# Fillers between SBUF pools, a token-major last projection, and 64x64 steps on four quarters of the array

## The chip, the cores and the metric

The kernel runs on one core of a Trainium2 chip. The metric is the device time of one execution in microseconds; the time of a kernel is the median over runs. An execution is also recorded by the hardware profiler, which gives the start and length of each instruction on five engines: TensorE (PE, and PEld for its weight loads), VectorE (DVE), ScalarE (ACT), GpSimd (POOL) and SyncE (SP), which issues most transfers.

## What is computed

A trunk of two decoder layers over 256 tokens of 2048 channels. Layer 0 mixes by stick-breaking attention and a gated delta rule, layer 1 by latent attention and gated linear attention; both go on with cross-attention to a memory of 256 rows and a convolutional feed-forward network (FFN) of 5632 hidden channels. Cut to what the change touches:

```python
def conv_ffn(h, w_in, conv_w, conv_b, w_out):
    uz = causal_dwconv(h @ w_in, conv_w) + conv_b
    u, z = jnp.split(uz, 2, axis=-1)
    return (jax.nn.silu(z) * u) @ w_out
...
    # gated_delta_rule, chunks of c = 64 tokens
    t_inv = jnp.eye(c, dtype=f32) + neg_n
    p = neg_n
    for _ in range(c.bit_length() - 2):
        p = p @ p
        t_inv = t_inv + t_inv @ p
...
    for layer in range(DEPTH):
        hn = rmsnorm(h, norm_mix[layer])
        ...
        h = h + memory_cross_attention(rmsnorm(h, norm_xattn[layer]), mem_n, ...)
        h = h + conv_ffn(rmsnorm(h, norm_ffn[layer]), ffn_w_in[layer], ...)
    return rmsnorm(h, final_norm)
```

## The kernel before

**Layout.** Activations lie channel-major: a tile has 128 channels on the partitions and the 256 tokens along the row. The residual stream is the 16 tiles X[0] to X[15].

**Exactness.** Every float32 factor is split into a rounded high part and a low remainder, and the products high x high, high x low and low x high are summed. An activation tile of 512 columns (xs, hid, mix, ms) holds 256 high and 256 low columns side by side. `get` brings half a slab of weights (128 x 1024) by a transfer on SP's queue into one of five raw buffers; ACT casts it to hi (L240), DVE subtracts to get lo in two halves (L249, from `low`). Four buffers of hi and of lo run ahead of TensorE.

**The main loop.** `mm_tile` keeps a 128x128 block of weights stationary and moves activations: for each block one matmul of 512 columns with hi (L277) and one of 256 with lo (L278), summed in a PSUM tile g. These two are called a pair here. `gemm` does 16 pairs for one output tile of 128 channels. `mm_narrow` does the same with three matmuls of 256 columns (L287 to L289). `gemm_b` is the other way about: a 128-token tile of activations is stationary and 512 weight columns move, three matmuls for each k and token tile (L326, L327, L329); it makes token-major results, in the value projections alone.

**The FFN.** `ffn` works in four groups of 11 hidden tiles. `into` makes a group: 22 output tiles of 16 pairs each, convolution, silu, product, and the split result hid0 to hid10. `out` then multiplies the group by the second weight matrix: 16 output tiles of 11 pairs, each added to X by `residual` (L416, L418). The last tile of all uses `mm_narrow`.

**The end.** `Final.feed` squares each finished X tile and multiplies it by the gain (ACT), POOL sums the squares; after the last tile TensorE sums over the partitions (L388), `rsqrt` works on 128x256 elements, 16 multiplications (L1264) follow, and eight transfers (L1265) write the channel-major result, which is transposed after the run.

**The delta rule.** `delta_pair` handles two heads; each head has two tiles t of two 64-token chunks. In six steps `it` it squares a 64x64 matrix and accumulates the inverse. Both chunks of a tile lie on the diagonal quarters of the array: rows and columns 0 to 63, and 64 to 127 (`halves`). For each step the code issues head 0's eight matmuls (L671 or L673, then L678 or L680), then head 1's; ACT copies (L692) and DVE adds (L694).

**Order.** Such side work is a generator; `Side` advances it as the pairs go by (`side.tick`, a `yield n` is n ticks), and the framework's scheduler then orders the instructions of each engine from its own estimates, so neighbours in the code need not be neighbours on the engine. Each engine runs its list in that order.

**Memory.** Pools are laid out one after another: constants and X (cp), xs and the like (xp), weights raw, hi, lo (wp), temporaries (tp), then the pools of a stage (mix's, the FFN's fp). A tile's size is rounded up to 32 bytes a partition, so a pool's start modulo 128 follows from what lies before it.

Of the kernel before, what the change touches and what calls it, by code (L numbers as in the profile page):

```python
# [10 lines left out]
F32 = mybir.dt.float32  # L11
# [7 lines left out]
P = 128  # L19
# [6 lines left out]
FG = 4  # L26
# [12 lines left out]
for _name, _c in SLABS:  # L39
# [6 lines left out]
    ("nm0", 16), ("nm1", 16), ("nx0", 16), ("nx1", 16), ("nf0", 16), ("nf1", 16), ("mem", 16), ("fin", 16),  # L46
# [101 lines left out]
def build(tc, nc, a):  # L148
# [87 lines left out]
    def part(raw):  # L236

        n = raw.shape[-1]
        hi, lo = parts()
# [5 lines left out]
    def parts():  # L245
        return [wp.tile([P, 1024], F32R, name=n, bufs=4) for n in ("hi", "lo")]
# [6 lines left out]
    def get(i, h, keep=None):  # L253
        if (i, h) not in cache:
# [7 lines left out]
            cache[i, h] = part(raw)  # L262
# [91 lines left out]
    class Norm:  # L354


        def __init__(self, d, name="R", bufs=2, p=None, cols=False):
            self.d, self.name, self.bufs, self.p, self.r = d, name, bufs, p, None
            self.acc, self.last, self.cols = {}, [], cols
# [22 lines left out]
        def get(self):  # L382
            if self.r is None:
                n = 258 if self.cols else 256
                ps = acc()
                z = list(self.acc.values()) + self.last
# [55 lines left out]
    def even():  # L442
# [143 lines left out]
        def delta_pair(h0, kq0s, vs, sgts):  # L586
# [63 lines left out]
            for i in two:  # L650
# [5 lines left out]
                for r in halves:  # L656
                    V.tensor_tensor(out=n[r, :, 2], in0=p3[r, :, r], in1=C["I64"][r, 0:64].unsqueeze(1).to_broadcast([64, 2, 64]), op=ALU.add)
                sts.append(n)
            yield 6

            full = [None, None]
            for it in range(6):
                p2s = [acc() for _ in two]
                c0, c1 = (1 if it < 4 else 2), (3 if it > 0 else 2)
                for i in two:
                    p3 = p2s[i][:, 0:384].rearrange("p (t c) -> p t c", t=2)
                    st = sts[i]
                    for t in range(2):
                        for r in halves:
                            if it == 0:  # L670
                                T.matmul(p3[r, t, 64:128], lhsT=p0[i][r, t, r], rhs=pt[i][r, t, r], start=True, stop=True)  # L671
                            else:
                                T.matmul(p3[r, t, 64 * c0:64 * c1], lhsT=st[r, t, 0], rhs=st[r, t, c0:c1], start=True, stop=True)  # L673
                    if it < 5:
                        for t in range(2):
                            for r in halves:
                                if it == 0:
                                    T.matmul(p3[r, t, 0:64], lhsT=pt[i][r, t, r], rhs=p0[i][r, t, r], start=True, stop=True)  # L678
                                else:
                                    T.matmul(p3[r, t, 0:64], lhsT=st[r, t, 1], rhs=st[r, t, 0], start=True, stop=True)  # L680
                for i in two:
                    p3 = p2s[i][:, 0:384].rearrange("p (t c) -> p t c", t=2)
                    st = sts[i]
                    if it == 5:
                        full[i] = vec("U")
                        G.memset(full[i], 0.0)
                        for r in halves:
                            V.tensor_tensor(out=full[i][r, :, r], in0=p3[r, :, 128:192], in1=st[r, :, 2], op=ALU.add)
                        continue
                    n = st if it == 0 else e("st", (P, 2, 3, 64), 4)  # L690
                    c = 2 if it < 4 else 1
                    A.copy(n.rearrange("p t q n -> p t (q n)")[:, :, 0:64 * c], p3[:, :, 0:64 * c])  # L692
                    if it:
# [489 lines left out]
    def ffn(l, nxt, after):  # L1183
        fp, es = open_pool("fp")
        e = maker(fp)
        xs, nm = nxt.xs, nxt.nm
# [29 lines left out]
        def out(gi, hid, nxt=None):  # L1216
            for n in range(16):
                ps = psum_g()
                f = [(gi * 16 + n) * FJ + k for k in range(FJ)]
                last = l == 1 and gi == FG - 1 and n == 15  # L1220
# [160 lines left out]
```

## Time and profile before

| | |
|---|---|
| time, median of 3 runs | 2589.1 us (2588.49 to 2589.78) |
| the profiled execution | 2590.2 us |
| its span, first to last instruction | 2588.4 us |
| TensorE matmuls | 15195, on 99% of the span |
| read from HBM | 453.28 MB, 176 GB/s |
| transfers of 512 KB of weights | 845, 3.3 us to landing each |

The page gives busy times, the chain of work that ended last (each step followed back to what released it), and groups of equal instructions: line, engine, operation, output and inputs, count, then busy time, mean length in ns, and idle time ahead of them with its releasers. Lengths of matmuls overlap, since a matmul starts before the one ahead has drained; what a matmul costs is the distance between starts. The FFNs run from 645 to 1373 us and from 1834 to 2574 us of the span.

### The profile page before, as it was taken

What the parts mean: (1) busy time and instruction counts of PE and PEld (TensorE: products, weight loads), DVE (VectorE), ACT (ScalarE), POOL (GpSimd) and SP (SyncE); (2) the same over time, 40 slices, a digit from 0 to 9 for tenths busy, and PEclk for the clock granted to TensorE, in tenths of its full rate; (3) what the DMA queues carried; (4) which work ended last, traced back from release to release, by engine and by line L of the source; (5) the groups of instructions that cost most, each with busy time, mean ns of one, the idle gap of its engine ahead of it and who ended that gap; (6) DMA issues with size and microseconds to landing.
All of it is one profiled execution on the core that took longest, in us unless ns stands there. A gap on an engine that the chain in (4) does not pass through costs nothing.

```text
span 2588.4 us, 41299 instructions
## 1 busy us (share of the span) xinstructions
PE 2560.0 (99%) x15195; PEld 2228.8 (86%) x15195; DVE 1972.0 (76%) x4050; ACT 1485.5 (57%) x2522; POOL 175.6 (7%) x240
## 2 busy tenths in 40 slices
PE   9999999999999999999999999999999999999997
PEld 7888888888888888888888888888988888888886
DVE  8888776877877767767777677876877777777766
ACT  7677656655655545545456555755655545535544
POOL 2001000302000000000011012120200000000001
PEclk9999999999999999999999999999999999999999
DMA  7333345654555555555555544465555555555553
GB/s 244 127 119 123 123 153 173 211 180 157 195 189 193 188 188 187 189 187 186 190 188 185 188 159 151 141 210 171 172 190 192 188 193 184 186 193 183 185 195 123
DMA packets 127548, 458.08 MB, mean 177 GB/s; under 512 B 14288, under 2 KB 14928, under 8 KB 127344
## 3 DMA queue, kind: packets, MB, share of 16 engines
q1 hardware_dynamic: 126000, 453.59, 52.7%
q8 instruction: 119, 1.95, 0.3%
q10 hardware_dynamic: 1344, 1.84, 0.2%
q14 instruction: 85, 0.70, 0.1%
HBM read 453.28 MB, written 2.10 MB: 176 GB/s over the span
## 4 chain that ended last, share of the span: by engine, by line
PE 92%; DVE 5%; ACT 2%; issue 1%; POOL 0%; DMA 0%; SPq 0%; DVEq 0%; ACTq 0%; POOLq 0%
PE g L277 53%; PE g L278 27%; PE g L326 2%; PE g L329 2%; PE g L327 2%; DVE lo L249 2%; DVE xs L231 1%; PE ps_a L673 1%; DVE cv L548 1%; DVE X L416 0%; ACT hi L240 0%; PE ps_a L1170 0%; PE ps_a L613 0%; PE ps_a L680 0%; PE ps_a L1135 0%
## 5 line engine op out<-in xcount | busy, mean ns | idle before, releaser
L249 DVE TENSOR_TENSOR lo<-raw,hi 128x512 fp32r<-128x512 f32 (+1 forms) x1697 | 1172.2, 705 | 477.0 <-ACT hi L240 462.7
L277 PE MATMUL g<-xs,hi 128*128 128x512 f32 x4112 | 1457.1, 398 | 2.3 <-DVE xs L231 2.1
L240 ACT CAST hi<-raw 128x1024 fp32r<-128x1024 f32 (+1 forms) x847 | 888.9, 1051 | 821.6 <-PE g L277 528.7
L278 PE MATMUL g<-xs,lo 128*128 128x256 f32 x4112 | 1154.7, 281 | 0.0
L277 PEld LDWEIGHTS g<-xs,hi 128*128 128x128 f32 x4112 | 771.7, 188 | 184.0 <-DVE xs L231 4.2
L278 PEld LDWEIGHTS g<-xs,lo 128*128 128x128 f32 x4112 | 776.0, 189 | 2.7 <-DVE lo L249 0.6
L277 PE MATMUL g<-hid,hi 128*128 128x512 f32 x1397 | 484.6, 392 | 0.0
L278 PE MATMUL g<-hid,lo 128*128 128x256 f32 x1397 | 390.5, 280 | 0.0
L277 PEld LDWEIGHTS g<-hid,hi 128*128 128x128 f32 x1397 | 262.3, 188 | 58.0
L278 PEld LDWEIGHTS g<-hid,lo 128*128 128x128 f32 x1397 | 262.3, 188 | 0.0
L370 POOL TENSOR_TENSOR sqacc<-sqacc,sq 128x256 f32<-128x256 f32 x129 | 115.7, 901 | 1981.6 <-ACT sq L369 1974.8
L277 PE MATMUL g<-mix,hi 128*128 128x512 f32 x508 | 178.6, 394 | 0.0
L1198 DVE SCALAR_TENSOR_TENSOR fc<-y,cg,fc 128x255 f32<-128x255 f32 x352 | 168.0, 478 | 0.1
L278 PE MATMUL g<-mix,lo 128*128 128x256 f32 x508 | 142.1, 280 | 0.0
L337 DVE TENSOR_TENSOR y<-g,t 128x256 f32<-128x256 f32 x285 | 118.7, 417 | 4.7 <-ACT t L335 4.2
L416 DVE TENSOR_TENSOR X<-g,X 128x256 f32<-128x256 f32 x192 | 80.2, 419 | 47.9 <-PE g L278 41.7
L277 PEld LDWEIGHTS g<-mix,hi 128*128 128x128 f32 x508 | 95.2, 187 | 22.6
L335 ACT COPY t<-g 128x256 f32<-128x256 f32 x285 | 103.1, 362 | 6.4 <-PE g L278 6.1
L1196 ACT ACTIVATE fc<-y,cg 128x256 f32<-128x256 f32 x176 | 105.3, 599 | 2.2 <-DVE y L1194 2.2
L278 PEld LDWEIGHTS g<-mix,lo 128*128 128x128 f32 x508 | 95.2, 187 | 0.0
L1194 DVE TENSOR_TENSOR y<-y,R 128x256 f32<-128x256 f32 x176 | 73.3, 417 | 0.1
L230 ACT ACTIVATE xs<-X,cg 128x256 fp32r<-128x256 f32 x96 | 47.6, 506 | 40.2 <-DVE X L418 25.6
(357 smaller groups left out, 2295.7 us busy)
## 6 DMA issues: line engine op xcount, KB each, us to landing
raw<-w SPq DMA_DIRECT2D x845, 512.0 KB, 3.3
raw<-mem SPq DMA_DIRECT2D x8, 512.0 KB, 3.5
X<-x SPq DMA_DIRECT2D x8, 256.0 KB, 5.7
out<-xg SPq DMA_DIRECT2D x4, 256.0 KB, 2.3
out<-xg ACTq DMA_DIRECT2D x4, 256.0 KB, 2.5
raw<-w SPq DMA_DIRECT2D x2, 384.0 KB, 5.1
cg<-cg SPq DMA_DIRECT2D x1, 599.5 KB, 8.9
raw<-w SPq DMA_DIRECT2D x2, 256.0 KB, 4.4
```

The costliest lines, as they stand in the source:

```text
L240: A.copy(hi[:, 0:n], raw)
L249: V.tensor_tensor(out=lo[:, s], in0=raw[:, s], in1=f32(hi[:, s]), op=ALU.subtract)
L277: T.matmul(ps[0:m, 0:512], lhsT=hi[:, w], rhs=xs[k], start=first and q == 0, stop=False)
L278: T.matmul(ps[0:m, 0:256], lhsT=lo[:, w], rhs=xs[k][:, 0:256], start=False, stop=last and q == n - 1)
L326: T.matmul(ps[t], lhsT=xh, rhs=hi[:, w], start=k == 0, stop=False)
L335: A.copy(t[0:m], ps[0:m, 256:512])
L337: V.tensor_tensor(out=y[0:m], in0=ps[0:m, 0:256], in1=t[0:m], op=ALU.add)
L370: eng.tensor_tensor(out=self.acc[eng], in0=self.acc[eng], in1=q, op=ALU.add)
L416: V.tensor_tensor(out=X[n], in0=ps[:, 0:256], in1=X[n], op=ALU.add)
L1194: V.tensor_tensor(out=y, in0=y, in1=R, op=ALU.mult)
L1196: A.activation(c, y, AF.Identity, scale=col(f"fc{l}", n * 3 + 2), bias=col(f"fb{l}", n))
L1198: V.scalar_tensor_tensor(out=c[:, s:], in0=y[:, 0:S - s], scalar=col(f"fc{l}", n * 3 + 2 - s), in1=c[:, s:], op0=ALU.mult, op1=ALU.add)
```

## The change

Three things are changed. First, unused tiles (`fill`) of 32, 96 and 64 bytes are put into the pools xp, wp and tp, and 64 into the second FFN's pool; hi and lo get 1056 columns for 1024, and where weights move, the data starts 8 columns (32 bytes) in (`skew`). With the 16 gain columns that leave the constants this sets the addresses modulo 128 bytes: xs from 0 to 96, hi and lo from 0 to 64, hid from 32 to 96, and mix at 96.

```diff
+    def fill(p, n):
+        p.tile([P, n // 4], F32, name="fill", bufs=1)
+    fill(xp, 32)
+    fill(wp, 96)
+    fill(tp, 64)
+    SKEW = 8
-        hi, lo = parts()
+        hi, lo = [x[:, skew:skew + n] for x in parts()]
-        return [wp.tile([P, 1024], F32R, name=n, bufs=4) for n in ("hi", "lo")]
+        return [wp.tile([P, 1056], F32R, name=n, bufs=4) for n in ("hi", "lo")]
...
-            hi, lo = get(base + k // 4, k % 4 // 2)
+            hi, lo = get(base + k // 4, k % 4 // 2, skew=SKEW)
```

Second, the second FFN's output projection is token-major. `turn` transposes X into two token tiles XB during the first group; `out_b` replaces `out`: for each of four column tiles c of 512 channels and each k, three matmuls for each of two token tiles, weights moving. `finish` squares with a sum along the row, multiplies by the gain, and after the last column tile works out the norm on 128x1 elements, scales and writes rows of the result. In the last column tile the first token tile's last six k come ahead of the second's.

```diff
+        def turn():
+            for c in range(4):
+                for t in range(2):
+                    yield 6
+                    ps = acc()
+                    for i in range(4):
+                        T.transpose(ps[:, i * P:i * P + P], X[4 * c + i][:, t * P:t * P + P], ident)
+                    A.copy(XB[t][:, c], ps)
+            side.spawn(turn())
...
+            for c in range(4):
+                ps = [psum_g() for _ in range(2)]
+                steps = [(k, t) for k in range(FJ) for t in range(2)]
+                if end and c == 3:
+                    steps.sort(key=lambda s: (min(s[0], FJ - 6), s[1], s[0]))
+                for k, t in steps:
...
+                    T.matmul(ps[t], lhsT=xh, rhs=hi[:, w], start=k == 0, stop=False)
+                    T.matmul(ps[t], lhsT=xh, rhs=lo[:, w], start=False, stop=False)
+                    T.matmul(ps[t], lhsT=xl, rhs=hi[:, w], start=False, stop=k == FJ - 1)
+                    if k == FJ - 1:
+                        x = XB[t][:, c]
+                        V.tensor_tensor(out=x, in0=ps[t], in1=x, op=ALU.add)
+                        if end:
+                            finish(t, c, x)
...
+            q = e("fq", (P, 512), 2)
+            A.activation(q, x, AF.Square, accum_out=sums[:, t, c:c + 1])
+            o = xp.tile([P, 512], F32, name="xg", tag="xs", bufs=16)
+            (V if c == 3 else G).tensor_tensor(out=o, in0=x, in1=gb[:, c], op=ALU.mult)
+            fin[t, c] = o
+            if c == 3:
+                n = tmp("n", (P, 1), 2)
+                V.tensor_reduce(out=n, in_=sums[:, t], axis=AX.X, op=ALU.add)
+                z = rsqrt(n, 1, 1.0 / D, r[:, t:t + 1])
+                for i in range(4):
+                    o = fin[t, i]
+                    if i % 2:
+                        A.activation(o, o, AF.Identity, scale=z)
+                    else:
+                        V.tensor_scalar(out=o, in0=o, scalar1=z, scalar2=None, op0=ALU.mult)
+                    (nc.scalar if i % 2 else nc.sync).dma_start(a["out"][t * P:t * P + P, i * 512:i * 512 + 512], o)
```

Third, in `delta_pair` head 1's matrices change halves at each step (rows r, columns and output w = the other half), so that its matmuls use the two quarters of the array off the diagonal, and the code interleaves the heads.

```diff
+                for t in range(2):
+                    for i in two:
+                        for b in range(2):
+                            r, w = halves[b], halves[b ^ i]
...
+                                T.matmul(p2s[i][w, t, 64 * c0:64 * c1], lhsT=sts[i][r, t, 0], rhs=sts[i][r, t, c0:c1], start=True, stop=True)
...
+                        elif it and i:
+                            V.tensor_tensor(out=n[w, :, 2], in0=p3[w, :, 128:192], in1=st[r, :, 2], op=ALU.add)
-                    if it:
+                    if it and it < 5 and i == 0:
                         V.tensor_tensor(out=n[:, :, 2], in0=p3[:, :, 128:192], in1=st[:, :, 2], op=ALU.add)
```

In the order of TensorE, the second pair of heads (st holds a head's matrices, p_1909 head 1's first one, xs the gemm's activations), before:

```order
L671 MATMUL ps_a<-pt,p_1909 64x64 x4
L678 MATMUL ps_a<-p_1909,pt 64x64 x4
L673 MATMUL ps_a<-st 64x128 x4
L680 MATMUL ps_a<-st 64x64 x4
L278 MATMUL g<-xs_209,lo 128x256
L673 MATMUL ps_a<-st 64x128 x4
L680 MATMUL ps_a<-st 64x64 x4
L277 MATMUL g<-xs_216,hi 128x512
```

and the same place now:

```order
L683 MATMUL ps_a<-pt,p_1916 64x64 x4
L691 MATMUL ps_a<-p_1916,pt 64x64 x4
L685 MATMUL ps_a<-st 64x128 x4
L693 MATMUL ps_a<-st 64x64 x4
L288 MATMUL g<-xs_212,lo 128x256
L685 MATMUL ps_a<-st 64x128 x4
L693 MATMUL ps_a<-st 64x64 x4
L287 MATMUL g<-xs_219,hi 128x512
```

The lines have moved (L673 is now L685, L680 is L693, L277 is L287), the order has not: four matmuls of one head follow each other, on two quarters. In the fourth pair of heads, now:

```order
L685 MATMUL ps_a<-st 64x128 x8
L693 MATMUL ps_a<-st 64x64 x8
L288 MATMUL g<-xs_226,lo 128x256
L287 MATMUL g<-xs_233,hi 128x512
L288 MATMUL g<-xs_233,lo 128x256
L287 MATMUL g<-xs_240,hi 128x512
L685 MATMUL ps_a<-st 64x128 x4
L693 MATMUL ps_a<-st 64x64
L685 MATMUL ps_a<-st 64x128 x4
L693 MATMUL ps_a<-st 64x64 x7
```

Here eight follow each other, of both heads, on four quarters; that holds for three steps of this pair. In all, the steps stand in 35 runs between the gemm's matmuls where they stood in 34.

On DVE, the end of the program before (rs_v, rs_q and R are the norm's values, xg the results):

```order
L343 TENSOR_SCALAR rs_v<-ps_a 128x256
L349 SCALAR_TENSOR_TENSOR rs_q<-rs_q,rs_v 128x256
L351 SCALAR_TENSOR_TENSOR R<-rs_q,rs_y 128x256
L1264 TENSOR_TENSOR xg_26823<-xg_26823,R 128x256 x2
L1264 TENSOR_TENSOR xg_26903<-xg_26903,R 128x256 x2
```

with six more such rows behind these, and now:

```order
L1298 TENSOR_SCALAR xg<-xg,rfin 128x512 x2
L1277 TENSOR_TENSOR xb_19935<-g,xb_19935 128x512
L1287 TENSOR_TENSOR xg<-xb_19935,gb 128x512
L1291 TENSOR_REDUCE n<-sums 128x1
L353 TENSOR_SCALAR rs_v<-n 128x1
L359 SCALAR_TENSOR_TENSOR rs_q<-rs_q,rs_v 128x1
L361 SCALAR_TENSOR_TENSOR rfin<-rs_q,rs_y 128x1
L1298 TENSOR_SCALAR xg<-xg,rfin 128x512 x2
```

The first row is the first token tile's scaling, and the second tile's add (L1277), which waits for the last matmul, stands behind it.

More of the change, by code (lines that the diff above doesn't have):

```diff
@@ L234, in xs_tile, with part @@
         return p.tile([P, 512], F32R, name=name, tag=tag, bufs=bufs)
-    def part(raw):
+    def part(raw, skew=0):
         n = raw.shape[-1]
-        hi, lo = parts()
+        hi, lo = [x[:, skew:skew + n] for x in parts()]
         A.copy(hi[:, 0:n], raw)
@@ L261, in get @@
                 raw = load(a[i][:, h * n:h * n + n])
-            cache[i, h] = part(raw)
+            cache[i, h] = part(raw, skew)
             if keep is not None:
@@ L662, in delta_pair @@
             for it in range(6):
-                p2s = [acc() for _ in two]
+                p2s = [acc()[:, 0:384].rearrange("p (t c) -> p t c", t=2) for _ in two]
                 c0, c1 = (1 if it < 4 else 2), (3 if it > 0 else 2)
-                for i in two:
[L666 to L680, printed above, removed]
@@ new lines, in delta_pair @@
+                for t in range(2 if it < 5 else 0):
+                    for i in two:
+                        for b in range(2):
+                            r, w = halves[b], halves[b ^ i]
+                            if it == 0:
+                                T.matmul(p2s[i][w, t, 0:64], lhsT=pt[i][r, t, r], rhs=p0[i][r, t, r], start=True, stop=True)
+                            else:
+                                T.matmul(p2s[i][w, t, 0:64], lhsT=sts[i][r, t, 1], rhs=sts[i][r, t, 0], start=True, stop=True)
@@ L684, in delta_pair @@
+                for i in two:
+                    p3, st = p2s[i], sts[i]
+                    n = None
                     if it == 5:
-                        full[i] = vec("U")
+                        full[i] = e("U", (P, 2, P), 2, tag="p0")
                         G.memset(full[i], 0.0)
[L687 to L690, printed above, removed]
@@ L1219, in out @@
                 f = [(gi * 16 + n) * FJ + k for k in range(FJ)]
-                last = l == 1 and gi == FG - 1 and n == 15
-                (mm_narrow if last else mm_tile)(ps, [(OFF[f"fo{l}"] + i // 16, i % 16, k) for k, i in enumerate(f)], hid)
-                residual(n, ps, nxt, last)
+                mm_tile(ps, [(OFF[f"fo{l}"] + i // 16, i % 16, k) for k, i in enumerate(f)], hid)
+                residual(n, ps, nxt)
+        if l == 1:
+            XB = [e(f"xb{t}", (P, 4, 512)) for t in range(2)]
+            gb = e("gb", (P, 4, 512))
+            nc.sync.dma_start(gb, a["fin"])
+            def turn():
[7 more added lines that the diff above has]
+            side.spawn(turn())
+            sums, r = e("sums", (P, 2, 4)), e("rfin", (P, 2))
@@ L1228, in ffn @@
             nxt = into(gi)
[L1229 removed]
+            side.drain()
+            (out_b if l else out)(gi - 1, prev)
             prev = nxt
         use_table("natural_log_exp_and_others")
[L1232 removed]
+        if l:
+            out_b(FG - 1, prev)
+        else:
+            out(FG - 1, prev, after)
         es.close()
[L1235 to L1250 removed]
     mixed = even()
@@ L1259, in build @@
     nxt = cross(1, mixed)
-    fin = Final()
-    ffn(1, nxt, fin)
-    for k, o in enumerate(fin.xg):
-        for i in range(2):
-            (G if k in (3, 6) and i else V).tensor_tensor(out=o[:, i], in0=o[:, i], in1=fin.nm.R, op=ALU.mult)
-        (nc.scalar if k % 2 else nc.sync).dma_start(a["out"][:, 2 * k:2 * k + 2], o)
+    ffn(1, nxt, None)
     st.close()
@@ L1331, in layout @@
         parts[f"fi{l}"] = _lay_a(I["ffn_w_in"][l], KD)
-        parts[f"fo{l}"] = _lay_fo(I["ffn_w_out"][l])
+        parts[f"fo{l}"] = (_lay_fo_b if l else _lay_fo)(I["ffn_w_out"][l])
     for n, c in SLABS:
```

66 lines of the change are left out of this document (36 added, 30 removed).

## The prediction

> **What bounds the kernel now.** I read the busy times first, then the chain that ended last, then its costliest groups.
>
> ```profile
> PE 2560.0 (99%) x15195; PEld 2228.8 (86%) x15195; DVE 1972.0 (76%) x4050; ACT 1485.5 (57%) x2522; POOL 175.6 (7%) x240
> PE 92%; DVE 5%; ACT 2%; issue 1%; POOL 0%; DMA 0%; SPq 0%; DVEq 0%; ACTq 0%; POOLq 0%
> L277 PE MATMUL g<-xs,hi 128*128 128x512 f32 x4112 | 1457.1, 398 | 2.3 <-DVE xs L231 2.1
> L278 PE MATMUL g<-xs,lo 128*128 128x256 f32 x4112 | 1154.7, 281 | 0.0
> L277 PE MATMUL g<-hid,hi 128*128 128x512 f32 x1397 | 484.6, 392 | 0.0
> L277 PE MATMUL g<-mix,hi 128*128 128x512 f32 x508 | 178.6, 394 | 0.0
> L249 DVE TENSOR_TENSOR lo<-raw,hi 128x512 fp32r<-128x512 f32 (+1 forms) x1697 | 1172.2, 705 | 477.0 <-ACT hi L240 462.7
> ```
>
> TensorE carries 92% of the chain and waits for nearly nothing. So time moves only with what a matmul costs from one start to the next, and with what stands before the first and after the last. The means of 398 and 281 ns cannot price that, because matmuls overlap: a pair (512 moving columns on hi, then 256 on lo) would be 679 ns by them. I therefore count the L277 records in long stretches. A record overlaps the edges, so one of the count is taken off.
>
> ```profile
> 660.00:880.00 220.00, 220.00 (x636) 1.00 0.57 190
> 944.00:1063.00 119.00, 119.00 (x338) 1.00 0.56 186
> 1130.00:1248.00 118.00, 118.00 (x335) 1.00 0.56 187
> 1254.00:1372.00 118.00, 118.00 (x341) 1.00 0.57 187
> 1860.00:2078.00 218.00, 218.00 (x630) 1.00 0.58 191
> 2144.00:2264.00 120.00, 120.00 (x340) 1.00 0.55 185
> 2330.00:2450.00 120.00, 120.00 (x341) 1.00 0.55 185
> 2456.00:2569.00 113.00, 113.00 (x327) 1.00 0.50 167
> 446.60:533.90 87.30, 86.64 (x249) 1.00 0.64 207
> 941.00:1065.00 124.00, 124.00 (x704) 107.49 (x703) 93.98 (x193) 69.65 (x106) 0.00 (x0) 1.00 0.56 184
> ```
>
> Each row is a stretch, its length, TensorE's busy time with the count, granted clock, DMA share and GB/s (the last row: PE, PEld, DVE, ACT, POOL). The clock is 1.00 throughout. Where hid moves (1254:1372, 2456:2569) a pair takes 118/340 = 347.1 and 113/326 = 346.6 ns. Where xs moves there are two paces: 220/635 = 346.5 and 218/629 = 346.6, but 119/337 = 353.1, 118/334 = 353.3, 120/339 = 354.0 and 120/340 = 352.9. Once slow, xs stays slow for a whole stretch of 352 pairs. With mix it is 86.64/248 = 349.4; I use 350.1, between this and its twin stretch in the odd layer. In the last row DVE is busy 94.0 and ACT 69.7 of 124 us: a pace faster by 2% fits under both.
>
> **The fillers.** In the addresses of the built program, taken modulo 128 bytes, hi and lo lie at 0; the moving rows lie 0 from them for xs, 32 for hid and ms, 96 for mix. After the change every xs, hid, mix and ms pair has 32. The rows above say what that buys if the distance decides: the fast pace, 346.7, always. Four of the eight xs stretches of the two FFNs are slow, 22 x 16 = 352 pairs each: 4 x 352 x (353.3 - 346.7) = 9.3 us. The other 4112 - 8 x 352 = 1296 xs pairs lie in broken stretches that I cannot count cleanly; between none and all of them slow is 0 to 8.6 us, and I take the half that the FFNs show, 4.3. Mix: 508 x (350.1 - 346.7) = 1.7 us.
>
> Where weights move instead (gemm_b, L326 to L329, three matmuls of 512 columns), the pace is read from starts four rounds apart:
>
> ```profile
> 428.21 0.39 PE L326 MATMUL g<-hi,xs 128*128 128x512 f32 x1
> ...
> 430.93 0.39 PE L326 MATMUL g<-hi,xs 128*128 128x512 f32 x1
> ...
> 600.15 0.40 PE L326 MATMUL g<-hi,ms 128*128 128x512 f32 x1
> ...
> 602.96 0.40 PE L326 MATMUL g<-hi,ms 128*128 128x512 f32 x1
> ```
>
> With xs stationary (distance 0) a round takes 2.72/4 = 680 ns, with ms (distance 96) 2.81/4 = 702 ns. The skew puts ms and Rk at distance 0: 64 + 16 rounds x 22 ns = 1.8 us. Fillers together: 9.3 + 4.3 + 1.7 + 1.8 = **17.1 us less**.
>
> The Trainium skill speaks against this part. In "SBUF — State Buffer", section "Who interferes with whom", it gives TensorE one read port for the moving operand and an independent one for LDWEIGHTS, and says that PE never waits on anyone. By that rule the distance would change nothing and the sum would lack these 17.1 us. No run here shows the ports; the rows of 353 ns beside 346.6 show that something slows the stream.
>
> **The last projection, token-major.** Before, an output tile of 512 channels by 256 tokens took, for each k, four pairs: 4 x 346.7 = 1387 ns. Now it takes two rounds of three matmuls of 512 columns with weights moving, at distance 0. I take the round of gemm_b, 680 ns: 1360. That is 27 ns x 11 x 4 x 4 = 176 steps = **4.7 us less**. The other end is the round of 702: 1404, or 3.0 us more. Its 32 adds of 512 columns take the place of 128 of 256 on DVE, and the squares, gains and sums of Final leave ACT and POOL; TensorE covers both. The feed is no bound: a half slab now lasts 2 x 1360 = 2720 ns, in which DVE needs two of the 705 ns. In the last column of tiles the six last k run for one token tile and then for the other, so three half slabs are wanted in 18 x 227 ns = 4.1 us; four buffers hold them.
>
> X has to be turned first: 32 transposes in 8 groups, during the first input group of the last FFN. The nearest group of four:
>
> ```profile
> 578.46 0.29 PE L278 MATMUL g<-xs,lo 128*128 128x256 f32 x1
> 578.58 0.60 PE L1149 MATMUL ps_a<-cg,xsc 128*128 128x128 f32 x4
> 578.94 0.47 PE L277 MATMUL g<-xs,hi 128*128 128x512 f32 x1
> ```
>
> From the first transpose to the next pair are 0.36 us, and that pair's first matmul is 0.08 longer (0.47 for 0.39): 0.44 x 8 = **3.5 us more** (2.9 if the longer record costs nothing). The 8 copies on ACT and the 1 MB of gains on SP hide under the ACT share and five raw buffers; SP's order has eight loads of weights ahead of the gains, so a wait there finds the buffers full.
>
> **The 64x64 steps.** In before, two quarters of the array run at once and the two heads follow each other:
>
> ```profile
> 241.51 0.65 PE L673 MATMUL ps_a<-st 64*64 64x128 f32 x8
> 242.00 0.40 PE L680 MATMUL ps_a<-st 64*64 64x64 f32 x8
> 242.23 0.61 PE L673 MATMUL ps_a<-st 64*64 64x128 f32 x8
> 242.67 0.40 PE L680 MATMUL ps_a<-st 64*64 64x64 f32 x8
> 243.00 0.39 PE L278 MATMUL g<-xs,lo 128*128 128x256 f32 x1
> L688 DVE TENSOR_TENSOR U<-ps_a,st 64x128 f32<-64x128 f32 x16 | 4.6, 287 | 2.0 <-PE ps_a L673 1.4 <-issue 0.3
> ```
>
> Two heads' step takes 243.00 - 241.51 = 1.49 us, the second head's part 0.67 (0.44 from 242.23 to 242.67, and 0.23 for its L680, as from 242.00 to 242.23). But the code's interleaving survives in the order only for three steps of the last pair of heads; everywhere else the heads' matmuls still stand in blocks of four on two quarters. So 3 x 0.67 = 2.0 us at most can be hidden there, and a wave of 0.1 us at some ten places where one head's block meets the other's. Against it stand 35 blocks between the gemm's matmuls for 34, and for the second head two half additions where one whole stood, in four steps of each pair of heads: 16 more on DVE, ahead of that head's next matmuls. If TensorE waited for each, that is 16 x 0.287 = 4.6 us (the nearest half addition, L688); the gemm's matmuls between the steps should cover most. I take **1.5 us less**; bounds 3 less and 4.6 more.
>
> The Trainium skill ("TensorEngine Tiling (Array Packing)", "Theoretical Speedup") gives up to four times for four 64x64 tiles; by it the two heads' steps would overlap wherever the order lets them, and the sum would take the bound of 3 us. No run here shows four quarters at once yet.
>
> **The end.** Before:
>
> ```profile
> 2573.57 0.28 PE L289 MATMUL g<-hid,lo 128*128 128x256 f32 x1
> 2573.89 0.42 DVE L416 TENSOR_TENSOR X<-g,X 128x256 f32<-128x256 f32 x1 [2.99 <-PE g L289]
> 2578.34 5.84 DVE L1264 TENSOR_TENSOR xg<-xg,R 128x256 f32<-128x256 f32 x14
> L1018 ACT ACTIVATE ex<-ps_a 128x512 f32<-128x512 f32 x8 | 4.8, 600 | 7.6 <-PE ps_a L1016 7.5
> L1141 ACT ACTIVATION_READ_ACCUMULATOR xsc<-ps_a,xmx x16: 192/196/203, 569.6 to 1791.1; 128x1 f32 x16
> L431 ACT ACTIVATE bt<-bt x1: 199/199/199, 54.7 to 54.7; 128x16 f32<-128x16 f32 x1
> L430 DVE TENSOR_SCALAR bt<-ps_a x1: 163/163/163, 53.4 to 53.4; 128x16 f32<-128x16 f32 x1
> ```
>
> From the last matmul's end, 2573.87, to the span's end, 2588.4, are 14.5 us; the multiplications end at 2584.2, so output and close take 4.2. Now, behind the last matmul: an add of 512 columns, 0.70 (as L249); square 0.60 and accumulator 0.20; reduce and three more tiny DVE steps 4 x 0.17, three tiny ACT steps 3 x 0.20; some ten hand-overs of 0.03; two scalings of 512 on each of two engines, 1.2; two issues on one queue where one stood last, 0.35; then the same 4.2. Sum 8.8. The second tile's add stands on DVE behind the first tile's scalings, and that chain, begun 4.1 us earlier, ends about when the last matmul does; I add 0.4: 9.2, **5.3 us less**. With the seven tiny steps as long as their 256-column forms in before (0.42) it would be 3.6, without the 0.4 and the accumulator 5.9.
>
> **Sum.** -17.1 - 4.7 + 3.5 - 1.5 - 5.3 = -25.1 us. The profiled execution took 2590.2 us (span 2588.4); the median of the three runs is 2589.1, so I subtract from that: **2564.0 us**.
>
> **Rivals.** (a) *Distance is not what decides.* For it: xs runs at both paces with the same distance 0, so something else chooses between them. Against it: hid at 32 ran fast in both quoted stretches, right after slow xs. Then the fillers' 17.1 fall away, and 8.0 remain: 2581. The Trainium skill's rule of independent ports, above, would make it so. (b) *The moving rows' own place decides.* In before hi and lo always lie at 0, so for pairs place and distance cannot be told apart; after, xs, hid and mix all lie at 96, where mix ran at 350.1. If place 96 costs 350.1, xs stays at its mean of 350.0, mix as it is, and the 704 hid pairs of the first FFN lose 3.4 each: 2581.1 + 2.4 = 2583.5. (c) *Slower*: the same mechanism with the slow pace of 353.3 at place 96, for 4112 + 704 + 508 pairs: 4112 x 3.3 + 704 x 6.6 + 508 x 3.2 = 19.8 us more, against 8.0 less from the other parts: 2600.9. The 5324 pairs cost 349.6 now on average, and 8.0 us are 1.5 ns each, so it decides from 351.1 on. For it: nothing but that mix lies there; against: gemm_b's pace changes while its moving rows stay at place 0. (d) *The token-major round locks into 702 ns*: 7.7 us worse, 2572. (e) *The four quarters overlap more than the order suggests, the end is shorter*: 2558.
>
> **Chances.** Forecast 0.64 (2556 to 2572), (a) 0.11, (b) 0.06, (c) 0.05, (d) 0.11, (e) 0.03. Range 2553 to 2581: it holds the forecast, (d), (e) and the lower half of (a). A measurement of this kernel tells about 0.2%, 5.2 us, from no change. Faster by more than that (below 2583.9) are the forecast, (d), (e), most of (a) and half of (b), with a little off for what no case holds: 0.87. Within it lie the rest of (a) and (b), 0.07; slower is (c) and a little, 0.06.
>
> **What will show it.** Fillers: L287 counts of 346.7 ns a pair in every xs stretch of both FFNs; 353 anywhere refutes the distance. Projection: rounds of 680 ns. Transposes: eight groups of 0.44 us. 64x64: blocks of 1.49 us everywhere but in the last pair of heads. End: some 9 us from the last matmul to the span's end. A DVE wait ahead of L1273, or TensorE idle in the even layer for the second head's additions, would make the prediction wrong in a way that no term holds.

## The result, and the profile after

The changed kernel takes 2573.55 us (median of 4 runs, 2573.30 to 2573.76) where the kernel before took 2588.8 us in the same job: a ratio of 0.994, 95% interval 0.9928 to 0.9951, or 15.3 us less. The forecast was 25.1 less, 2564.0 us. The time lies inside the range of 2553 to 2581; the sign and most of the means were right, the size was not.

The profiled execution took 2573.3 us. Its page, with the busy times, the chain and the costliest groups:

```profile
span 2571.5 us, 40527 instructions
...
PE 2547.2 (99%) x14860; PEld 2215.9 (86%) x14860; DVE 1944.5 (76%) x3968; ACT 1485.5 (58%) x2521; POOL 172.8 (7%) x230
...
PE 92%; DVE 4%; ACT 2%; issue 0%; POOL 0%; DMA 0%; ACTq 0%; POOLq 0%
...
L287 PE MATMUL g<-xs,hi 128*128 128x512 f32 x4112 | 1446.3, 394 | 1.2 <-DVE xs L241 1.0
...
L1272 PE MATMUL g<-hi,hid 128*128 128x512 f32 x352 | 138.0, 392 | 0.0
```

Nothing has become a new bound: the chain is TensorE's as before, and the new projection's matmuls (L1272) wait for nothing. So the difference is again one of paces and of the end. Cut at marks that both kernels have (matmuls at which one kind gives way to another), the span goes like this; the columns are lengths in us.

| stretch of the span | before | after | difference |
|---|---|---|---|
| start and even layer, to the first mix pair | 441.74 | 440.23 | -1.51 |
| even layer's mix projection | 92.40 | 91.64 | -0.76 |
| cross-attention 0 | 100.12 | 99.68 | -0.44 |
| FFN 0 | 738.69 | 734.74 | -3.95 |
| odd layer | 263.11 | 261.88 | -1.23 |
| its mix projection | 98.73 | 98.03 | -0.70 |
| cross-attention 1 | 100.07 | 99.70 | -0.37 |
| FFN 1, to the end of the last matmul | 738.99 | 736.38 | -2.61 |
| end | 14.56 | 9.19 | -5.37 |

The sum is 16.9. The profiled execution of before lay 1.4 above its median in that job and that of the changed kernel 0.25 below its own, so the medians differ by 15.3.

**The fillers** removed the slow stretches, as forecast. L287, counted in stretches as before (two in FFN 0 and one in FFN 1 where xs moves, then one where hid moves):

```profile
960.00:1050.00 90.00, 90.00 (x261) 1.00 0.58 192
1145.00:1235.00 90.00, 90.00 (x261) 1.00 0.58 190
2170.00:2250.00 80.00, 80.00 (x231) 1.00 0.58 191
1270.00:1360.00 90.00, 90.00 (x260) 1.00 0.56 186
```

90/260 is 346.2 and 80/230 347.8 ns a pair; a count of whole records is good to 0.4% here, and the starts of 33 pairs at a time give 347.1 nearly everywhere in the FFNs and in the mix projections, with no stretch of 353. But 347.1 is also what the pairs take that took 346.7 before.

**The token-major projection** did not. Its rounds are counted at L1272, the first of three matmuls, from the first to the last in groups three and four:

```profile
2440.61:2561.43 120.82, 68.61 (x175) 1.00 0.49 162
```

In this stretch are 175 rounds: 120.82/175 = 690.4 ns, not 680. They come in two kinds, some 680 and some 695 to 704. Sorting the single matmuls by the addresses of the built program gives the reason to test: hi and lo have buffers of 1056 columns, 4224 bytes, which is 128 modulo 256. So each second buffer lies 128 from the stationary rows modulo 256, the others 0, though all of them are at 0 modulo 128. At 0 a matmul of 512 columns takes 227.4 ns to the next start (527 of them), at 128 233.0 (526).

**The transposes.** The first of eight groups (L1253) with the matmuls around it:

```profile
1828.18 0.39 PE L287 MATMUL g<-xs,hi 128*128 128x512 f32 x1
1828.41 0.28 PE L288 MATMUL g<-xs,lo 128*128 128x256 f32 x1
1828.52 0.60 PE L1253 MATMUL ps_a<-cg,X 128*128 128x128 f32 x4
1828.88 0.47 PE L287 MATMUL g<-xs,hi 128*128 128x512 f32 x1
1829.19 0.28 PE L288 MATMUL g<-xs,lo 128*128 128x256 f32 x1
```

From the transposes to the next pair is 0.35 or 0.36 us in each group, 2.84 for eight. The first matmul behind them has a longer record (0.47) and delays the next start too: 0.31 us from L287 to L288 (1829.19 - 1828.88), where the pair ahead has 0.23. That is 0.09 in each group, and the eight cost 3.5 us. The stretch in which they stand grew by less, from 246.0 us in the kernel with the fillers alone (experiment 3) to 248.7, because a wait went: before, TensorE waited 0.78 us for xs, 6 us into this stretch.

```profile
1841.31 0.50 PE L277 MATMUL g<-xs,hi 128*128 128x512 f32 x1 [0.78 <-DVE xs L231]
```

Now two groups of transposes stand ahead of that matmul, and no wait of TensorE's for xs is left there.

**A step of the 64x64 work**, the one that took 1.49 us before:

```profile
242.47 0.65 PE L685 MATMUL ps_a<-st 64*64 64x128 f32 x8
242.96 0.22 PE L693 MATMUL ps_a<-st 64*64 64x64 f32 x2
242.97 0.33 PE L685 MATMUL ps_a<-st 64*64 64x128 f32 x2
243.02 0.34 PE L693 MATMUL ps_a<-st 64*64 64x64 f32 x5
243.13 0.27 PE L685 MATMUL ps_a<-st 64*64 64x128 f32 x1
243.14 0.22 PE L693 MATMUL ps_a<-st 64*64 64x64 f32 x1
243.14 0.49 PE L685 MATMUL ps_a<-st 64*64 64x128 f32 x5
243.46 0.40 PE L693 MATMUL ps_a<-st 64*64 64x64 f32 x8
243.79 0.51 PE L288 MATMUL g<-xs,lo 128*128 128x256 f32 x2
```

243.79 - 242.47 = 1.32 us. The heads overlap here although each head's matmuls stand together. In the last pair of heads, where eight matmuls of both heads alternate in the order, such a step takes 1.01 us (309.87 - 308.86):

```profile
308.86 0.73 PE L685 MATMUL ps_a<-st 64*64 64x128 f32 x14
...
309.87 0.38 PE L288 MATMUL g<-xs,lo 128*128 128x256 f32 x1
```

All blocks of such matmuls together take 28.73 us for 30.34; of the 1.61, the last pair of heads has 0.79.

**The end**, from the last matmul on (the chain of small steps, shortened; the first row is the first token tile's scaling):

```profile
2561.29 0.88 DVE L1298 TENSOR_SCALAR xg<-xg,rfin 128x512 f32<-128x512 f32 x2
...
2561.90 0.40 PE L1274 MATMUL g<-hi,hid 128*128 128x512 f32 x1
2562.33 0.69 DVE L1277 TENSOR_TENSOR xb<-g,xb 128x512 f32<-128x512 f32 x1 [0.16 <-PE g L1274]
2563.06 0.63 ACT L1285 ACTIVATE fq<-xb 128x512 f32<-128x512 f32 x1 [0.45 <-DVE xb L1277]
...
2563.81 0.16 DVE L1291 TENSOR_REDUCE n<-sums 128x1 f32<-128x4 f32 x1
...
2564.19 0.20 ACT L355 ACTIVATE rs_y<-rs_v 128x1 f32<-128x1 f32 x1 [0.41 <-DVE rs_v L353]
...
2565.35 1.33 ACT L1296 ACTIVATE xg<-xg,rfin 128x512 f32<-128x512 f32 x2 [0.48 <-DVE rfin L361]
2566.10 0.95 ACTq L1299 DMA_DIRECT2D out<-xg  x2
```

The last matmul ends at 2562.3, and the span at 2571.5: 9.2 us, as forecast. That it fits to the tenth is luck. The 0.4 that the forecast added because the second tile's add stands behind the first tile's scalings did not come: they end at 2562.17, before the last matmul. In its place ACT's two scalings took 1.33 us for 1.2, and issue, writes and close 4.8 (2566.68 to 2571.5) for 4.55.

**Waits in the even layer.** The prediction held that TensorE waits for nearly nothing. TensorE's three longest waits up to the first mix pair, before and then after (each row: instruction, what it waited for, us in total, times, longest):

```profile
PE ps_a L583 <- DVE rs_v L343: 6.2, 4, 2.4
PE ps_a L583 <- ACT sg L433: 2.2, 3, 0.8
PE ps_a L613 <- DVE kq L603: 2.0, 2, 1.0
```

```profile
PE ps_a L593 <- DVE rs_v L353: 5.1, 4, 1.4
PE ps_a L623 <- DVE kq L613: 2.6, 3, 1.0
PE ps_a L593 <- ACT sg L443: 2.4, 3, 0.8
```

They sum up to 10.4 and 10.1 us. L593 (L583 before) sums the squares of q and k; all three stand in the side work of the heads. That is 0.4% of the span, but it lies in the one stage where the 64x64 steps run.

### The profile page after: what moved, and what is told of

It reads as the page before. It is cut to its first block, busy times and chain, and to the rows that moved or that the text cites. A ratio compares the mean times of both kernels' runs of the same rounds, so it can differ in the third digit from the quotient of the medians.

```text
span 2571.5 us, 40527 instructions
## 1 busy us (share of the span) xinstructions
PE 2547.2 (99%) x14860; PEld 2215.9 (86%) x14860; DVE 1944.5 (76%) x3968; ACT 1485.5 (58%) x2521; POOL 172.8 (7%) x230
## 4 chain that ended last, share of the span: by engine, by line
PE 92%; DVE 4%; ACT 2%; issue 0%; POOL 0%; DMA 0%; ACTq 0%; POOLq 0%
PE g L287 47%; PE g L288 24%; PE g L1274 3%; PE g L1273 3%; PE g L1272 3%; PE g L336 2%; PE g L339 2%; PE g L337 2%; DVE lo L259 1%; DVE cv L558 1%; PE ps_a L685 1%; DVE xs L241 0%; PE g L298 0%; PE g L297 0%; PE g L299 0%
## 5 line engine op out<-in xcount | busy, mean ns | idle before, releaser
L287 PE MATMUL g<-xs,hi 128*128 128x512 f32 x4112 | 1446.3, 394 | 1.2 <-DVE xs L241 1.0
L288 PE MATMUL g<-xs,lo 128*128 128x256 f32 x4112 | 1157.1, 282 | 0.0
L287 PEld LDWEIGHTS g<-xs,hi 128*128 128x128 f32 x4112 | 771.6, 188 | 168.3 <-DVE xs L241 3.4
L288 PEld LDWEIGHTS g<-xs,lo 128*128 128x128 f32 x4112 | 774.1, 188 | 2.7 <-DVE lo L259 0.6
L287 PE MATMUL g<-hid,hi 128*128 128x512 f32 x704 | 244.5, 391 | 0.0
L288 PE MATMUL g<-hid,lo 128*128 128x256 f32 x704 | 197.6, 281 | 0.0
L380 POOL TENSOR_TENSOR sqacc<-sqacc,sq 128x256 f32<-128x256 f32 x115 | 104.7, 915 | 1256.9 <-ACT sq L379 1253.6
L287 PE MATMUL g<-mix,hi 128*128 128x512 f32 x508 | 177.1, 392 | 0.0
L287 PEld LDWEIGHTS g<-hid,hi 128*128 128x128 f32 x704 | 132.1, 188 | 28.8
L288 PE MATMUL g<-mix,lo 128*128 128x256 f32 x508 | 142.9, 281 | 0.0
L1274 PE MATMUL g<-hi,hid 128*128 128x512 f32 x352 | 138.1, 392 | 0.0
L1273 PE MATMUL g<-lo,hid 128*128 128x512 f32 x352 | 138.0, 392 | 0.0
L1272 PE MATMUL g<-hi,hid 128*128 128x512 f32 x352 | 138.0, 392 | 0.0
L288 PEld LDWEIGHTS g<-hid,lo 128*128 128x128 f32 x704 | 132.6, 188 | 0.0
L287 PEld LDWEIGHTS g<-mix,hi 128*128 128x128 f32 x508 | 95.4, 188 | 20.5
L288 PEld LDWEIGHTS g<-mix,lo 128*128 128x128 f32 x508 | 95.7, 188 | 0.0
```

The lines of the kernel that those rows point to most:

```text
L287: T.matmul(ps[0:m, 0:512], lhsT=hi[:, w], rhs=xs[k], start=first and q == 0, stop=False)
L288: T.matmul(ps[0:m, 0:256], lhsT=lo[:, w], rhs=xs[k][:, 0:256], start=False, stop=last and q == n - 1)
L380: eng.tensor_tensor(out=self.acc[eng], in0=self.acc[eng], in1=q, op=ALU.add)
L1272: T.matmul(ps[t], lhsT=xh, rhs=hi[:, w], start=k == 0, stop=False)
L1273: T.matmul(ps[t], lhsT=xh, rhs=lo[:, w], start=False, stop=False)
L1274: T.matmul(ps[t], lhsT=xl, rhs=hi[:, w], start=False, stop=k == FJ - 1)
```

## Experiments

Each kernel's time stands beside runs of the kernel before in the same job; times of different jobs are not subtracted. The pace of a pair is the mean distance between its start and the next pair's; pairs with other work between them (over 375 ns) are left out. Distances are from the addresses of the built programs: moving rows minus the stationary rows loaded next, now modulo 256. Except at the change from one buffer to the next, the stationary rows in use lie at the same distance, so the runs do not tell which of the two counts.

**1. All buffers at 128.** The changed kernel, one line:

```diff
-        return [wp.tile([P, 1056], F32R, name=n, bufs=4) for n in ("hi", "lo")]
+        return [wp.tile([P, 1088], F32R, name=n, bufs=4) for n in ("hi", "lo")]
```

> The changed kernel with its hi and lo tiles 1088 columns wide, so that every buffer of theirs starts at the same place modulo 256 bytes and, where weights move, the moving rows lie 128 from the stationary rows in every buffer (in the changed kernel by turns 0 and 128). Theory A, the distance counts modulo 256: every matmul of the last projection takes the 233.0 ns of the buffers at 128, a round 699 ns for the mean of 690, so 352 rounds x 9 ns = 3.2 us more, and up to 0.8 us more in the other matmuls with moving weights: 2577. Rival B, the distance counts modulo 128 only and the two paces come from something that alternates with the buffers (which tile is being filled, which half is read): the round stays at a mean of 690 with both paces, 2573.5. Pairs at 32 and 160 stay at 347 by both.

Measured: 2573.95 us (2573.31 to 2574.10). The rounds of L1272, from first to last:

```profile
2439.47:2561.47 122.00, 69.11 (x175) 1.00 0.50 161
```

122.00/175 = 697.1 ns: the fast kind is gone, all 1053 matmuls at 128 average 232.4. Theory A holds for the projection; 352 x 6.7 ns cost it 2.4 us. The total of 2577 did not come: it moved only 0.4, because pairs got faster at the same time, FFN 0 by 0.85 us. With all buffers alike, a pair takes 346.7 ns for 347.1, where the expectation had them stay at 347.

**2. All buffers at 0.** The width of 1088 and other fillers:

```diff
-    fill(wp, 96)
-    fill(tp, 64)
+    fill(wp, 224)
...
-        if l == 1:
-            fill(fp, 64)
+        fill(fp, 64 if l else 128)
...
-                n = tmp("n", (P, 1), 2)
+                n = e("nf", (P, 1), 2)
```

> The same width of 1088 columns, with the fillers set so that the last projection and the matmuls with moving weights on xs lie at 0 modulo 256 in every buffer (those on ms and on R at 128), pairs at 32 and 160 as before. Theory A, modulo 256: every matmul of the last projection takes 227.4 ns, a round 682 for 690, so 352 x 8 ns = 2.8 us less, and up to 0.8 less in the others: 2570. Rival B, modulo 128 only: a mean of 690 with both paces, 2573.5. If the place of the tiles decides by itself, whatever the distance, it would do what the run with all buffers at 128 does.

Measured: 2565.82 us (2565.70 to 2567.15), a ratio of 0.991 to before (0.9896 to 0.9923). The rounds, here at L1270:

```profile
2435.04:2554.05 119.01, 68.17 (x176) 1.00 0.50 164
```

With the last start on the window's edge it is 119.01/175 = 680.1 ns, with 330 of 349 at exactly 680. Theory A holds, and the prediction's 680 is the right price where its condition is met. In the same kernel gemm_b reads the same moving tiles against xs at 0 (228.0 ns) and against ms at 128 (232.8): one place, two distances, two paces. The total is better than the 2570 expected, by the 0.4 ns a pair above and by an even layer of 438.42 us for 440.23. Of these 1.8 us, 1.1 lie in one wait (L592 for sg, 1.3 us for 2.4) that differs by more between two runs of one kernel (see 9), so they are not put down to the distance.

**3. The fillers alone**, on the kernel before:

```diff
+    fill(xp, 96)
+    fill(wp, 96)
+    fill(tp, 128)
+    SKEW = 8
...
-        return [wp.tile([P, 1024], F32R, name=n, bufs=4) for n in ("hi", "lo")]
+        return [wp.tile([P, 1056], F32R, name=n, bufs=4) for n in ("hi", "lo")]
...
-                        full[i] = vec("U")
+                        full[i] = e("U", (P, 2, P), 2, tag="p0")
```

(with `part` and `get` taking the skew as in the change)

> The kernel before with the fillers, the skew and the tile width alone: no token-major projection, no four-quarter steps, the old end. Theory A, the distance decides the pace of pairs: xs, hid and mix all at 347.1 ns a pair, no stretch at 353; the two FFNs give 4.0 and about 4.0 us, the mixing projections 1.4, the cross-attentions 0.8, the odd layer 1.2, the even layer 0.5 to 1.5: 12 to 13 us below the kernel before, 2576. Rival C, the slow stretches went because of something else in the change (other code, other buffers in the last FFN): slow stretches of 353 remain, 2586 to 2589.

Measured: 2578.34 us against 2589.02, 10.7 less; by the spans of the profiled executions 11.3 less. Both FFNs give 3.9 to 4.0, the mix projections 0.78 and 0.69, the cross-attentions 0.9 together, the odd layer 1.3, the even layer nothing (+0.16). The paces are those of theory A, with no stretch at 353, and C falls; what is missing from A's 12 to 13 us is in the main the even layer's share. The fillers are two thirds of the change, and 17.1 was too much for them.

**4. The 64x64 steps of before**, in the changed kernel: the third part of the change undone, with U kept where the change puts it.

```diff
-                        for b in range(2):
-                            r, w = halves[b], halves[b ^ i]
...
-                                T.matmul(p2s[i][w, t, 64 * c0:64 * c1], lhsT=sts[i][r, t, 0], rhs=sts[i][r, t, c0:c1], start=True, stop=True)
...
+                                T.matmul(p3[r, t, 64 * c0:64 * c1], lhsT=st[r, t, 0], rhs=st[r, t, c0:c1], start=True, stop=True)
```

> The changed kernel with the 64x64 steps of before (two quarters, one head after the other, whole additions). Theory D, the steps are worth the 1.5 us predicted: the even layer is 1.5 us longer than in the changed kernel, 2575.0. Rival E, what the shorter blocks bring is lost in the longer gaps of the matmuls around them and in the half additions: the even layer is within 0.4 us of the changed kernel's, 2573.5. Rival F, the steps cost: the even layer is shorter by over 0.5 us, 2573 or less.

Measured: 2573.61 us (2573.38 to 2573.86). By the profiles the even layer is 0.62 us longer than in the changed kernel, and nothing else differs by 0.1. D and F fall; 0.62 is a little over what E allowed, and the time shows none of it. Where it comes from: blocks of 64x64 matmuls take 30.05 us here and 28.73 with the four quarters; but there are 32 blocks here and 35 there, and the distance from the gemm's last matmul ahead of a block to the block sums up to 4.09 and 4.67 us over its usual length. So 1.3 are won and 0.6 given back at the seams.

The kernel of 3 and this one differ in the even layer too, 441.90 and 440.84 us, though both have the fillers and neither has the new steps. These 1.06 us go with one wait, in 3 and then here:

```profile
PE ps_a L591 <- DVE rs_v L351: 6.4, 4, 2.5
```

```profile
PE ps_a L593 <- DVE rs_v L353: 5.1, 4, 1.3
```

Nothing in the change aims at it, and which of the other differences between the two kernels shortened it no run shows. So the 1.51 us of the even layer in the table, so close to the 1.5 forecast for the steps, are 0.6 of theirs and some 1.1 of this wait.

**5. The place, not the distance.** On the kernel before, an unused tile of 96 bytes ahead of xs, so that xs, hi and lo all move together:

```diff
+    xp.tile([P, 24], F32, name="fill", bufs=1)
```

> The kernel before with one filler of 96 bytes ahead of everything on its side: xs moves to the place 96 modulo 128, where it lies in the changed kernel, but its distance from hi and lo stays 0; hid goes from 32 to 160, and mix from 96 to 0. Theory A, the distance decides: xs still runs at two paces, stretches at 346.7 and stretches at 353.3, and mix, now at 0 too, at one of these: 2586 to 2592. Rival G, the own place of the moving rows decides (96 is fast, as everything lies there in the changed kernel): no stretch of xs at 353 is left, 2578 to 2580.

Measured: 2588.21 us (2586.07 to 2589.99). L279, in FFN 0, three stretches of xs and one of hid:

```profile
660.00:860.00 200.00, 200.00 (x578) 1.00 0.58 190
960.00:1050.00 90.00, 90.00 (x256) 1.00 0.57 187
1145.00:1235.00 90.00, 90.00 (x256) 1.00 0.57 187
...
1270.00:1360.00 90.00, 90.00 (x260) 1.00 0.57 187
```

200/577 = 346.6, 90/255 = 352.9 twice: the same stretches are slow as before. Mix, whose own tiles did not move but whose distance went from 96 to 0, now ran at 353.3 in the even layer and at 346.7 in the odd one, for 350.0 in both. G falls; the prediction's rivals (b) and (c) fall with it. (Modulo 256, hid lies 160 from hi and lo in both kernels; the expectation's 32 for before counts modulo 128.)

**6 to 8. Other distances for the pairs.** On the kernel before, an unused tile ahead of raw, hi and lo, of 128, 64 and 192 bytes:

```diff
+    wp.tile([P, 32], F32, name="fill", bufs=1)
```

(32 columns for 128 bytes, 16 for 64, 48 for 192)

> The kernel before with a filler of 128 bytes ahead of the raw, hi and lo tiles: xs lies 128 from hi and lo for 0, mix 224 for 96, hid 160 for 32; modulo 128 nothing changes. Theory A, pairs too count modulo 256: xs runs at a pace of its own, without the change between 346.7 and 353.3 from stretch to stretch; all fast it is 2580 (9 us from pairs less, and 356 matmuls with moving weights at 128, 4.8 ns each, 1.7 more: net 7 to 9), all slow 2604. Rival H, pairs count modulo 128: two paces by stretches as before and mix at 350, 2588 to 2592.

Measured: 2594.55 us, ratio 1.0021 (1.0011 to 1.003). xs at 128, L279:

```profile
660.00:860.00 200.00, 200.00 (x570) 1.00 0.57 188
...
1145.00:1235.00 90.00, 90.00 (x257) 1.00 0.56 187
```

200/569 = 351.5 and 90/256 = 351.6: one pace, 351.1 by the starts, in every stretch. Mix at 224 took 353.2 for 350.0 at 96. Theory A holds, H falls: for pairs too, distances that are equal modulo 128 can have different paces.

> The kernel before with a filler of 64 bytes there: xs lies 192 from hi and lo, mix 32, hid 160, all without the skew, so that matmuls with moving weights on xs lie at 64. Theory A with only the neighbourhood of 0 bad: xs pairs at 346.7 to 347.5 throughout, as at 32 and 160, 2577 to 2580. Rival I, 32 and 160 are good because they are odd multiples of 32: xs at 192 changes pace as it does at 0, 2587 to 2592.

Measured: 2599.17 us, ratio 1.0038 (1.0023 to 1.0053), slower than before. xs at 192:

```profile
660.00:860.00 200.00, 200.00 (x567) 1.00 0.57 187
...
1860.00:2060.00 200.00, 200.00 (x567) 1.00 0.57 187
```

200/566 = 353.4: always slow. Mix, now at 32, runs at 346.7. Both expectations fall: 192 is neither good nor of two paces.

> The kernel before with a filler of 192 bytes ahead of the raw, hi and lo tiles: xs lies 64 from hi and lo, mix and hid 160. Theory A2, pairs count modulo 256 and are slow from 96 to 128 and from 192 to 224 but fast in the 64 bytes above 0 and at 160: xs 346.7 throughout, mix 346.7, about 2579. Rival J, every even multiple of 32 is slow: xs at a constant pace of 350 to 353.3 like the runs at 128 and 192, 2589 to 2601. Mix at 346.7 for 350.0 gives 1.7 us less by both; the matmuls with moving weights on xs (at 192) lie between 228 and 233 ns.

Measured: 2591.76 us, but with runs from 2588.36 to 2594.73. xs at 64:

```profile
660.00:860.00 200.00, 200.00 (x567) 1.00 0.56 187
960.00:1050.00 90.00, 90.00 (x259) 1.00 0.57 190
```

353.4 in the first stretch, 90/258 = 348.8 later: two paces by stretches, as at 0. A2 falls, and J by the change of pace. Mix at 160 took 346.7, as said.

**9. At 0 on ms, too**, on the version of 2:

```diff
         op, es = open_pool("op")
+        fill(op, 128)
...
         ap, es = open_pool("ap")
+        fill(ap, 128)
```

> The version with all buffers at distance 0 in the last projection, and fillers in two more pools so that the matmuls with moving weights on ms lie at 0 too (those on R stay at 128). Theory A: 190 matmuls at 228 for 232.6 ns, 0.9 us less than that version, 2565.0; below both the kernel before and the changed one. If pace follows the kernel's stage and not the distance, 2565.8 as that version.

Measured: 2564.32 us, ratio 0.9904 (0.9887 to 0.9920). gemm_b's 530 matmuls at 0 take 227.9 ns. The cross-attentions are 0.6 and 0.7 us shorter than in the version of 2; the distance accounts for 0.5 of each (96 matmuls of 232.8 - 227.5 ns). The same kernel once more, in another job on the same chip:

> The fastest version so far again (fillers for distance 0 where weights move, pairs at 32 and 160), as the partner of the same version with the 64x64 steps of before: 2564.3.

Measured: 2565.99 us. The profiles of the two runs agree within 0.03 us in every stretch but the even layer, 437.98 and 439.65 us. One of TensorE's waits there has most of the difference, in the first run and then in the second:

```profile
PE ps_a L592 <- ACT sg L442: 0.7, 3, 0.3
```

```profile
PE ps_a L592 <- ACT sg L442: 2.5, 3, 0.8
```

Three waits are 0.6 us longer each. The same code falls into one or the other, so times of different jobs that differ by under 2 us tell no versions apart here, those of 2 and of 9 among them. With the version of 11 they are the fastest of this study, and beat both kernels: the version of 2 lies 7.8 us below the kernel of 4, which ran in its job and takes as long as the changed one.

**10. 16 bytes on.** The version of 9 with hi and lo read 4 columns further on where they are stationary:

```diff
-    def get(i, h, keep=None, skew=0):
+    def get(i, h, keep=None, skew=4):
```

> The fastest version so far (all buffers at 0 for moving weights, pairs at 32 and 160) with hi and lo read 16 bytes further on where they are stationary: xs, hid and ms pairs lie 16 away, mix 144. Theory A2: 16 and 144 lie between the good 32 and 160 and the unstable 0 and slow 128, so if the good places are narrow, pairs cost 350 to 353 and the time is 2581 to 2600; if they reach 16 bytes down, 2564.3 as that version.

Measured: 2581.47 us. L286, FFN 0 and FFN 1, the same kind of stretch:

```profile
660.00:860.00 200.00, 200.00 (x578) 1.00 0.56 191
...
1860.00:2060.00 200.00, 200.00 (x567) 1.00 0.56 187
```

At 16 xs has the two paces of 0, 346.6 in one FFN and 353.4 in the other; mix at 144 takes 353.3. Pairs at 16 and 144 lack the steady 346.7 of 32 and 160, so the good distances end within 16 bytes, and the time is the lower end of what was expected for that.

**11. The version of 9 with the 64x64 steps of before**, the edit of 4, in the same job as its partner above:

> The fastest version with the 64x64 steps of before. Theory E: the steps bring 0 to 0.6 us, as they did beside the changed kernel: 2564.3 to 2564.9, all of it in the even layer. Theory D: the 1.5 us of the prediction show where the gemm's matmuls around the steps run evenly: 2565.8. Theory F: the steps cost, 2563.8 or less.

Measured: 2566.02 us (2565.84 to 2566.89) against 2565.99. Against this partner E holds: by the profiles the even layer differs by 0.25 us, by the times not at all. The 2564.3 to 2564.9 that were expected did not come, since both ran with the longer even layer of 9.

## Why the prediction was right or wrong

By the profiled executions the 16.9 us are, in round figures: 11.3 from the fillers, 1.1 from the projection, 0.6 from the 64x64 steps, 5.4 from the end, 1.1 and 0.8 from two waits that shrank or went without being aimed at, less 3.5 for the transposes. The forecast had 17.1, 4.7, 1.5, 5.3, nothing for the waits, and 3.5.

**What bounds the kernel: right outside the even layer.** A pace that changes by 6 ns shows in the time in full in both FFNs. In the even layer TensorE waits some 10 us for the heads' side work before and after, and the fillers alone brought nothing there.

**The fillers: right in mechanism, mis-sized.** 17.1 were forecast; alone they brought 11.3 by the profiled executions and 10.7 by the times. The FFN term of 9.3 came out as 7.9: the slow stretches went, but the fast pairs went from 346.7 to 347.1, because the buffers of 1056 columns alternate between the distances 32 and 160. Mix was 1.5 for 1.7. The terms that failed are "other xs", 4.3, and gemm_b, 1.8. Together they stand against 2.0 in the cross-attentions, the odd and the even layer.

For "other xs" the half share of slow pairs, taken from the FFNs, was near: counted from start to start (those over 375 ns left out), the xs pairs outside the FFNs took 3.8 us more than at 346.7 before, and 0.8 more with the fillers alone. So 3.0 were to be had, and the 1.2 of them that lie in the even layer did not shorten it.

Gemm_b did not gain at all. Four rounds each gave 680 and 702 ns, 22 apart; over all rounds before, 356 matmuls at 0 took 228.2 and 211 at other distances 233.3 ns, which is 15 ns a round. And after, half of all, at 0, take 229.0 and half, at 128, take 232.4, which is 0.4 us more than before in all.

**The projection: the step that failed is "at distance 0".** The prediction took all addresses modulo 128, by which every buffer lies at 0, and priced every round at 680. Modulo 256 half of them lie at 128. The gain was 352 rounds of 690.4 against as many half steps of 693.4, 1.1 us, not 4.7. The runs with all buffers alike gave 697.1 and 680.1. Rival (d), a round of 702 throughout, was near for half of the buffers.

**The transposes: right, 3.5 us.** Both parts of the price came as forecast, 0.35 to the next pair and 0.09 behind it. That TensorE's wait for xs went at the same time was not forecast.

**The end: 5.4 for 5.3**, with two errors that cancel, as said above.

**The 64x64 steps: wrong in where, and too large.** The overlap was expected in the last pair of heads alone, up to 2.0 us; blocks shrank in all four pairs, by 1.6 us in sum, half of it in the last. But the seams took part of it back: 0 to 0.6 us were measured for 1.5. With four quarters a step of 1.49 us took 1.32 where the heads follow each other in the order and 1.01 where they alternate. That fits an overlap that the order limits, but no run changed the order alone. The feared half additions show in no wait of TensorE's.

**Rivals.** (a), that distance does not decide, falls: the same xs tiles at the same place have paces that change by stretches at distance 0, 351.1 throughout at 128 and 353.3 throughout at 192, while moving xs, hi and lo together changed no FFN stretch (5). Its argument stays open all the same: at 0 something else chooses between 346.7 and 353.3. The Trainium skill ("SBUF — State Buffer", "Who interferes with whom") has independent read ports for the moving rows and the weight loads, by which this would not happen. The measured paces decide against using that rule as a price here; what in the memory makes them differ no run shows.

## What to carry to other kernels

Price a matmul by the distance between starts, sorted by where its operands lie, and look for the period of the effect before building on it: here buffers that seemed aligned modulo 128 alternated modulo 256, and 32 more columns with other fillers brought 7.8 us more, half as much again as the change (1.8 of them in the even layer, where one code differs from itself by as much). Before crediting a faster step in a stage, read that stage's own waits: the even layer kept nothing of the 1.2 us won in its pairs and at most 0.6 of the 1.3 won in its steps, and got 1.1 from a wait that nobody aimed at.

## What the runs showed of the hardware

In these runs the pace of TensorE's matmuls goes with the distance between moving and stationary rows modulo 256 bytes. A dash: not measured with more than a few dozen matmuls.

| distance | a pair (512 and 256 columns moving), ns | 512 columns with weights moving, ns |
|---|---|---|
| 0 | 346.7 or 353.3, by stretches | 226.7 to 229.0 |
| 16 | 346.7 or 353.3, by stretches | - |
| 32 | 346.7 | - |
| 64 | 348.9 or 353.3, by stretches | 229.3 |
| 96 | 350.0 | 233.2 |
| 128 | 351.1 | 232.4 |
| 144 | 353.3 | - |
| 160 | 346.7 | - |
| 192 | 353.3 | 233.3 |
| 224 | 353.2 | - |

Of these distances only 32 and 160 are fast throughout for pairs, though 96 and 224 are odd multiples of 32 as well; for weights that move, 0 is the fastest. Where a distance has two paces, one of them holds in the FFNs for hundreds of pairs, and where it changes, other matmuls stood in between; what chooses it was not found. Whether it differs from one execution to the next was not seen, since one execution of each run was profiled; the kernel with xs at 64 ran between 2588.36 and 2594.73 us, which would fit.
